# Depthwise convolution of a Conformer mixer: the shifted copies made by products with the identity, and all 31 taps on TensorE

## Chip, cores and metric

The kernel runs on one core of a Trainium2 chip. The metric is the device time of one execution, in microseconds (us). Engines: TensorE (PE; PEld is its weight load), VectorE (DVE), ScalarE (ACT), GpSimd (POOL) and SyncE (SP), which issues most DMAs. ScalarE has a DMA queue of its own.

## The reference

Two layers on 256 tokens of 2048 channels, float32. Layer 0 mixes the tokens by a state-space model, layer 1 by a causal convolution; each mixer is followed by a SwiGLU FFN of 5632 hidden units, each sub-layer by a layer norm, with scales, shifts and gates from a modulation `silu(c) @ ada_w`. The change lies in the convolution mixer:

```python
def conv_mixer(u, w_pw1, w_dw, b_dw, g_norm, b_norm, w_pw2):
    d = u.shape[-1]
    ab = u @ w_pw1
    v = ab[..., :d] * jax.nn.sigmoid(ab[..., d:])
    v = lax.conv_general_dilated(v, w_dw[:, None, :], window_strides=(1,),
        padding=((CONV_WIDTH - 1, 0),), dimension_numbers=('NWC', 'WIO', 'NWC'),
        feature_group_count=d) + b_dw          # CONV_WIDTH = 31
    v = layer_norm(v, g_norm, b_norm)
    return jax.nn.silu(v) @ w_pw2
```

Each channel is convolved with 31 taps of its own along the tokens; token t sees tokens t-30 to t.

## The kernel before

Activations lie as [channel, token], the channels in 16 chunks of 128. Even tokens come before odd ones, except in the convolution, which takes them in their order.

**Dense products.** A weight is taken in units of 512 rows by 512 columns (1 MB). SyncE's queue loads a unit into one of the four buffers of the pool `raw` (L496); ScalarE casts it into `whi` (L805), VectorE subtracts to get `wlo` (L806), and `gemm` (L811) makes 48 matmuls of 128x128 by 128x256 from it (L850): hi by hi, hi by lo, lo by hi. `whi` and `wlo` have two buffers each, so the cast of a unit waits until the products of the unit two before it are done. A panel is 256 output channels of both halves of `w_pw1`, four units; the mixer has eight panels. Panel 0 comes through a path of its own (`Entry`, L952), which also makes the input for the others.

**Work between the units.** `Later` (L565) holds work that is due some units on; `gemm` calls it ahead of each unit. `AdaQueue` (L618) puts loads of the modulation's weights, 1 MB each, between the units (0.6 a unit in this stage), and VectorE adds them up (L674).

**The convolution.** Behind each panel `conv_in` (L1427) takes its two chunks of gated channels: ScalarE copies a chunk to a padded buffer `pad` (L1431). The products need a tile `vs` in which 32 channels stand on all four quarters of the partitions, a token later on each: with it a 128x32 block of weights `lw` takes four taps at a time. The tile is made by a trip through DRAM: ScalarE's queue writes `pad` to the scratch tensor `scr` (L1433, 139.5 KB) and, when that is done, reads it back in overlapping rows into `vs` (L1440, 556.5 KB). GpSimd makes `lw` (L1442). `conv_out` (L1463) makes 4 x 6 products of 128x32 by 128x256 a chunk (L1467), four of them, for the four quarters of channels, into one PSUM bank; they hold taps 0 to 23. `conv_taps` (L1448) makes the last seven taps on VectorE (L1454 to L1458), and VectorE adds both to `V` (L1471) and, through `Stats`, to the sums of the layer norm (L748, L750; `lnsum` L765). `conv_taps` is put off by one unit and `conv_out` by three in most panels, longer in panels 0, 1 and 6.

**Around it.** PSUM has three banks in the pool `aux` (L498), which convolution, turns and sums share. The engines' instructions run in an order that the framework's scheduler sets when it builds the kernel. Behind the last panel, `fill` (L1509) gives TensorE products of the modulation while the layer norm is made; two of their loads are issued on ScalarE's queue behind the last `vs` load.

Of the kernel before, what the change touches and what calls it, by code (L numbers as in the profile page):

```python
# [26 lines left out]
CONV_G = 6  # groups of four taps of the convolution on the tensor engine  # L27
# [25 lines left out]
class Ops:  # L53
    """Short names for elementwise operations on one engine."""
# [27 lines left out]
    def exp(self, out, x):  # L82
        """out = e**x to float32, over the whole range of x."""
# [20 lines left out]
    def sincos(self, s_out, c_out, x):  # L104
        """s_out, c_out = sin(x), cos(x), x reduced by multiples of pi/2 in exact pieces."""
# [40 lines left out]
def bc(ap, axis, n):  # L146
    """The AP with a broadcast axis of length n put in at axis."""
    a = ap.unsqueeze(axis)
    sh = list(a.shape)
    sh[axis] = n  # L150
    return a.broadcast_to(sh)


class S5:
    """Parameter tables and the scan of the diagonal state-space mixer.

    Two tokens a step: H_c = a^2 H_{c-1} + (a B u_{2c} + B u_{2c+1}), and y = Re(C f H) with f = (a - 1) / lam.
    The complex state is kept in a frame that turns by 2*phi a step, phi the angle of a, in which the
    recurrence has the real factor |a|^2 and its two parts are two real scans.
    States lie on partitions as (group parity, n), group pairs along the free axis.  # L160
    """

    def __init__(self, tc, const, ident, psum, psum_tag, psum2):
# [5 lines left out]
        # B and C, the latter with -Im  # L169
        self.cm = self.keep.tile([P, 4, NPAIR, GI], F32, name="cm")  # L170
        # quarters of the channels of a tile, at both tokens of a step
# [22 lines left out]
    def load(self, pp, lam_re, lam_im, log_dt):  # L194
        """Pairs of groups on partitions, real parts on the first half of them."""
        nc = self.nc
        self.ld = pp.tile([64, 2], F32, name="ld")
        self.lam = pp.tile([P, P], F32, name="lam")
        self.nat = [pp.tile([P, 2 * NS * GI], F32, name=f"nat{i}") for i in range(2)]
        nc.sync.dma_start(self.ld, log_dt.rearrange("o (j a) -> (o j) a", a=2))  # L200
        for r, t in enumerate((lam_re, lam_im)):
            nc.sync.dma_start(self.lam[64 * r:64 * r + 64], t.rearrange("(j a) n -> j (a n)", a=2))
# [22 lines left out]
    def turn_mats(self):  # L225
        nc, cm = self.nc, self.cm
        # B and C, states to the partitions
# [14 lines left out]
    def prep(self, pp):  # L242
# [6 lines left out]
        # angles phi and phi * 4, 16, 64, the products by powers of two being exact  # L249
# [29 lines left out]
        # rotation factors e^{i 2 phi 2^j}, the first 16 steps of the tables, and |a|^2 e^{i 2 phi 64}  # L279
# [19 lines left out]
    def matrices(self, q, eng):  # L299
        """B, a B, C f and C f a of a quarter of the group pairs, in steps."""  # L300
# [5 lines left out]
        # (real or imaginary, pair, token of a step, channel) and (matrix, pair, channel)  # L306
# [20 lines left out]
    def quarter(self, q):  # L327
        """The first 32 steps of the tables of a quarter of the group pairs."""
# [6 lines left out]
    def double(self, t, w, j, xt, yt, npair, eng=None):  # L335
        """t[2^j : 2^{j+1}] = t[:2^j] * w along the last axis; t, w as [re, im]."""
# [15 lines left out]
    def tables(self, ct):  # L352
        """Rotation tables and decay factors of channel tile ct (4 group pairs) over 64 steps."""
# [15 lines left out]
    def weights(self, ct):  # L369
        """The matrices of channel tile ct in the shapes that the tensor engine takes."""  # L370
# [12 lines left out]
        # (pair, token of a step, channel) to the partitions, two pairs at a time  # L383
# [16 lines left out]
    def drive(self, ct, u):  # L400
        """PSUM banks with a B u_{2c} + B u_{2c+1}, two pairs of groups each; u by halves of the channels.

        Each pair takes half of the rows of the array, so that two products run at a time.
        """
# [9 lines left out]
    def scan(self, ct, banks, tab, between):  # L414
        """The states' real and imaginary parts as products of the scans with the tables.

        The frame starts anew after 64 steps; the state is carried over. between() is called where other
        work fits between operations that need one another.
        """
# [43 lines left out]
    def read_out(self, ct, u, pc, psn):  # L463
        """PSUM bank with y[ch, (tau, c)] of the channels of tile ct, without D u."""
# [3 lines left out]
        # Re(C H): C_re (c g_re - s g_im) - C_im (c g_im + s g_re)  # L468
# [15 lines left out]
def kernel(  # L484
# [4 lines left out]
    """Activations lie as [channel, token], tokens ordered (t mod 2, t div 2).  # L489

    Products with the weights are float32 products of operands split as hi + lo, each of 12 bits:
    hi hi + lo hi + hi lo, in one pass each.
    """
# [61 lines left out]
    def load_unit(src, k0, kn, segs, eng=nc.sync):  # L555
        """Rows of 128-chunks k0..k0+kn of a weight, column ranges segs (512 columns in all)."""
# [8 lines left out]
    class Later:  # L565
        """Work put off by some units of the dense products, so that the tensor engine needn't wait for its inputs."""
# [20 lines left out]
    def queue_behind(instructions):  # L587
        """A context whose instructions are issued after these, each on its own engine."""
# [8 lines left out]
    def ada_block(layer, j, q, behind={}):  # L597
        """Columns q*512.. of part j of the modulation, in four units; scales and gates get their 1 added."""
# [19 lines left out]
    class AdaQueue:  # L618
        """The rest of the modulation on the vector engine, a unit of 128 rows and 2048 columns at a time.

        parts = (layer, part, first of 4 blocks of 512 columns): what is left of a part from this block on;
        with half of the columns a unit has 256 rows.
        """
# [8 lines left out]
        def run(self, marks=()):  # L632
            """Adds up what was loaded before, behind these instructions."""
# [17 lines left out]
        def step(self):  # L651
            """Loads a unit; returns what adds it up."""
# [47 lines left out]
    def inverse_std(v, y, hv, t):  # L700
        """y = 1 / std from half of the variance, to which half of the epsilon is added; t for between.

        A first value from the exponent (negative), then three steps of Newton, each of which turns the sign.
        """
# [8 lines left out]
    class Stats:  # L713
        """Sums over the channels of z and z*z, z less the mean of its first 256 channels.

        Each quarter of the tokens has its sums on a quarter of the partitions. apart: the last two
        chunks stay out of the sums.
        """
# [5 lines left out]
        def begin(self, z):  # L724
            """z [128, 2, 256]: channel chunks 0 and 1; rewritten less the shift."""
# [10 lines left out]
        def add(self, i, z):  # L736
            """z [128, 2, 256]: channel chunks 2i and 2i+1, less the shift."""
# [17 lines left out]
        def finish(self, fill=None):  # L755
            """PSUM bank with 1/std and mean/std of z, on every partition.

            fill makes products for the tensor engine to do while it waits, in two steps.
            """
# [30 lines left out]
    def normal(z, r):  # L790
        """z [128, n, 256] -> (z - mean) / std in place."""
# [5 lines left out]
    class Unit:  # L797
        """A unit of a weight, loaded and split."""
# [769 lines left out]
```

## Time and profile before

| | |
|---|---|
| times of three runs | 2469.03, 2470.73, 2472.2 us (median 2470.73) |
| the profiled execution | span 2466.8 us from the first to the last instruction; no other time of it is recorded |
| busy | PE 2272.2 us (92%), DVE 1713.9 (69%), ACT 993.7 (40%), POOL 265.1 (11%) |
| mean granted TensorE clock | 0.963 |
| convolution's products (L1467) | 768 records, first at 1292.5 us, last at 1565.3 |
| taps on VectorE (L1454) | 96 instructions, median 484 ns |
| DMA issues of ScalarE's queue | 16 to `scr`, 16 to `vs` |
| moved | 584.36 MB, mean 237 GB/s |

How to read it: the page gives busy times by engine and by groups of instructions, with the idle time ahead of each and what ended it. The view of waits lists who waited for whom, with total, count and longest. The busy time by stretches gives the same for a window of the span. A float32 product of TensorE shows as two records.

### The profile page before, as it was taken

The page shows a single profiled execution, that of the slowest core. Times are in us where ns is not written, and L with a number is a line of the kernel's source. Part 1 is how long each engine was busy: PE and PEld are TensorE (multiplying, and loading weights), DVE is VectorE, ACT ScalarE, POOL GpSimd, SP SyncE. Part 2 cuts the span into 40 slices and gives each one's busy share as a digit, 9 for nine tenths or more (in the row PEclk, how much of TensorE's full clock was granted, in tenths as well). Part 3 has the DMA queues.
Part 4 walks back from the last instruction along what each step waited for, and adds up shares of the span by engine and source line. Part 5 has one row for each costly group of instructions (what it writes and reads, how often), then busy time and mean ns, then how long its engine had stood idle before and what let it go on. Part 6 is the DMA issues. An engine that isn't in the chain of part 4 may idle for free.

```text
span 2466.8 us, 46658 instructions
## 1 busy us (share of the span) xinstructions
PE 2272.2 (92%) x20224; PEld 2136.9 (87%) x20224; DVE 1713.9 (69%) x1884; ACT 993.7 (40%) x1191; POOL 265.1 (11%) x249
## 2 busy tenths in 40 slices
PE   5767899999999999999977867699999999999998
PEld 2434799999999999999976756499999999999998
DVE  8999888787776777778776564588765544545564
ACT  3555333564333334334452222345533333333343
POOL 3575200110000000000021100402000000000000
PEclk7888999999999999999989988899999999999999
DMA  9766899578888888888756676674775555555542
GB/s 293 252 222 200 308 344 339 189 265 299 307 306 300 302 303 300 305 315 287 242 167 180 186 193 174 226 256 155 254 263 185 187 188 180 182 187 188 188 158 100
DMA packets 377620, 584.36 MB, mean 237 GB/s; under 512 B 17315, under 2 KB 269523, under 8 KB 362819
## 3 DMA queue, kind: packets, MB, share of 16 engines
q1 hardware_dynamic: 371686, 567.43, 68.6%
q10 hardware_dynamic: 5520, 13.58, 2.0%
q8 instruction: 158, 2.59, 0.4%
q0 software_dynamic: 208, 0.37, 0.1%
q14 instruction: 48, 0.39, 0.0%
HBM read 576.95 MB, written 4.38 MB: 236 GB/s over the span
## 4 chain that ended last, share of the span: by engine, by line
PE 70%; DVE 12%; DMA 8%; issue 6%; ACT 2%; POOL 2%; ACTq 0%; SPq 0%; DVEq 0%; POOLq 0%
PE acc L850 66%; DMA raw<-in_cv_w_pw_dram 4%; DMA scr<-pad 2%; DVE x L433 1%; DMA vs<-scr 1%; DVE x L426 1%; DVE wlo L806 1%; ACT whi L805 1%; POOL hl L935 1%; DVE pc L458 1%; DMA raw<-in_s_w_glu_dram 1%; DVE adaacc L674 1%; POOL hf L1506 0%; DVE x L430 0%; DVE ct L1454 0%
## 5 line engine op out<-in xcount | busy, mean ns | idle before, releaser
L806 DVE TENSOR_TENSOR wlo<-raw,whi 128x2048 fp32r<-128x2048 f32 x344 | 792.0, 2302 | 595.0 <-ACT whi L805 590.7
L805 ACT CAST whi<-raw 128x2048 fp32r<-128x2048 f32 x344 | 655.8, 1907 | 977.8 <-PE acc L850 618.0
L850 PE MATMUL acc<-hh,whi 128*128 128x256 f32 x3904 | 668.0, 283 | 34.3 <-ACT whi L805 31.1
L850 PE MATMUL acc<-hl,whi 128*128 128x256 f32 x3904 | 664.1, 283 | 0.0
L850 PEld LDWEIGHTS acc<-hh,whi 128*128 128x128 f32 x3904 | 552.4, 190 | 55.2 <-ACT whi L805 36.7
L850 PEld LDWEIGHTS acc<-hl,whi 128*128 128x128 f32 x3904 | 550.6, 190 | 1.0 <-issue 0.8
L850 PE MATMUL acc<-hh,wlo 128*128 128x256 f32 x3904 | 514.6, 282 | 4.4 <-DVE wlo L806 4.4
L850 PEld LDWEIGHTS acc<-hh,wlo 128*128 128x128 f32 x3904 | 485.8, 190 | 5.4 <-DVE wlo L806 5.4
L674 DVE SCALAR_TENSOR_TENSOR adaacc<-rawa,c_act,adaacc 128x2048 f32<-128x2048 f32 (+1 forms) x135 | 286.3, 2121 | 0.3
L850 PE MATMUL acc<-fh,whi 128*128 128x256 f32 x1408 | 237.5, 284 | 0.0
L850 PE MATMUL acc<-fl,whi 128*128 128x256 f32 x1408 | 236.7, 283 | 0.0
L850 PEld LDWEIGHTS acc<-fh,whi 128*128 128x128 f32 x1408 | 199.0, 192 | 0.9 <-ACT whi L805 0.8
L850 PEld LDWEIGHTS acc<-fl,whi 128*128 128x128 f32 x1408 | 198.9, 192 | 0.0
L850 PE MATMUL acc<-fh,wlo 128*128 128x256 f32 x1408 | 185.9, 283 | 0.0
L850 PEld LDWEIGHTS acc<-fh,wlo 128*128 128x128 f32 x1408 | 176.4, 192 | 0.0
L1442 POOL TENSOR_TENSOR lw<-fold,wtap 128x768 f32<-128x768 f32 x16 | 31.4, 1962 | 967.6 <-PE acc L850 721.2
L1467 PE MATMUL conv<-vs,lw 128*32 128x256 f32 x768 | 55.7, 450 | 62.6 <-DMA vs<-scr 62.6
L1467 PEld LDWEIGHTS conv<-vs,lw 128*32 128x32 f32 x768 | 28.5, 128 | 85.3 <-issue 63.8
L604 PE MATMUL ada<-raw,c_rep 128*32 128x512 f32 x512 | 79.8, 704 | 6.6 <-DMA raw<-in_ada_w_dram 6.5
L935 POOL TENSOR_TENSOR hl<-hf,hh 128x512 fp32r<-128x512 f32 x24 | 47.9, 2007 | 284.4 <-ACT hh L934 277.2
L1094 POOL CAST lnmh<-lno 128x2 fp32r<-128x2 f32 x1 | 0.2, 183 | 725.1 <-DVE lno L65 725.1
L1148 ACT ACTIVATE fsg<-acc 128x256 f32<-128x256 f32 x84 | 32.0, 381 | 108.4 <-PE acc L850 108.4
(318 smaller groups left out, 1705.3 us busy)
## 6 DMA issues: line engine op xcount, KB each, us to landing
raw<-in_ffn_w_gu_dram SPq DMA_DIRECT2D x352, 512.0 KB
rawa<-in_ada_w_dram SPq DMA_DIRECT2D x128, 1024.0 KB
raw<-in_ffn_w_down_dram SPq DMA_DIRECT2D x88, 1024.0 KB
raw<-in_ada_w_dram SPq DMA_DIRECT2D x62, 1024.0 KB
raw<-in_s_w_glu_dram SPq DMA_DIRECT2D x64, 512.0 KB
raw<-in_cv_w_pw_dram SPq DMA_DIRECT2D x64, 512.0 KB
raw<-in_cv_w_pw_dram SPq DMA_DIRECT2D x16, 1024.0 KB
vs<-scr ACTq DMA_DIRECT2D x16, 556.5 KB
```

The source lines that it names most:

```text
L426: v.tensor_tensor(out=dst.rearrange("p r s a c -> p a (r s) c")[:, a::2], in0=pv.rearrange("p a r (s c) -> p a (r s) c", s=2), in1=bc(f[:, ...
L433: v.tensor_tensor_scan(out=x2[:, r, s].rearrange("p a c -> p (a c)"), data0=rh.rearrange("p a c -> p (a c)"), data1=x1[:, r, s].rearrange( ...
L458: v.tensor_tensor(out=pc[:, r].rearrange("p a (s c) -> p s a c", s=2), in0=x2[:, r], in1=bc(t[:, 0], 1, 2), op=MUL)
L604: nc.tensor.matmul(acc[32 * k:32 * k + 32, :], c_rep[:, 4 * u + k, :], r[:, k, :], start=u == 0, stop=u == 3)
L674: nc.vector.scalar_tensor_tensor(out=acc, in0=r[:, i], scalar=c_act[:, kk:kk + 1], in1=acc, op0=MUL, op1=ADD)
L805: m1 = nc.scalar.copy(out=self.hi[:, :kn], in_=r[:, :kn])
L806: m2 = nc.vector.tensor_tensor(out=self.lo[:, :kn], in0=r[:, :kn], in1=self.hi[:, :kn].bitcast(F32), op=SUB)
L850: nc.tensor.matmul(acc[bank][:, i], wt[:, k, m * P:(m + 1) * P], xx(u0 + k), start=u == 0 and n == 0 and i == 0, stop=last and n == len(or ...
L935: nc.gpsimd.tensor_tensor(out=hl[:, s2], in0=h, in1=hh[:, s2].bitcast(F32), op=SUB)
L1148: nc.scalar.activation(out=t[:, i], in_=gv[:, 0], func=AF.Sigmoid)
L1442: nc.gpsimd.tensor_tensor(out=lw, in0=fold32.unsqueeze(1).unsqueeze(1).broadcast_to([P, 4, CONV_G, 32]), in1=bc(wtap[:, :, 4 * ch:4 * ch + ...
L1467: nc.tensor.matmul(acc[32 * q:32 * q + 32, :], lw[:, q, g, :], vs[:, LS * q + 4 * g:LS * q + 4 * g + SEQ], start=g == 0, stop=g == CONV_G - 1)
```

## The change

`CONV_G` becomes 8, so that the products take all 31 taps (the 32nd is zero) and `conv_taps` goes. The scratch tensor goes with both DMAs of each chunk. In their place `conv_spread` multiplies, for each quarter of the channels, 32 columns of the identity by the padded chunk at four shifts, each into a quarter of the partitions of a bank of `aux`, 284 tokens long; ScalarE copies the banks of two quarters to `vs`, VectorE those of the other two. The delays become one unit for `conv_spread` and two for `conv_out` (one more for a panel's second chunk), in every panel. `vs` has three buffers for four, `lw` three for two. All loads of `fill` go to SyncE's queue. The taps' table `wtap` is 8 groups wide; the table for VectorE, `vtap`, goes.

```diff
-CONV_G = 6  # groups of four taps of the convolution on the tensor engine
+CONV_G = 8
...
-        LS = 4 * CONV_G - 1 + SEQ
-        dramp = mctx.enter_context(tc.tile_pool(name="dram", bufs=1, space=bass.MemoryType.DRAM))
+        LS = 4 * CONV_G - 4 + SEQ
...
         def conv_in(i, t):
             p = pad[i % 2]
-            scr = []
             for k in range(2):
                 nc.scalar.copy(out=p[:, k, WIDTH - 1:LP - 1].rearrange("p (c t) -> p t c", t=2), in_=t[:, k].rearrange("p (t c) -> p t c", t=2))
-                scr.append(dramp.tile([32, 4, LS], F32, name=f"scr{2 * i + k}"))
-                m = nc.scalar.dma_start(scr[k].rearrange("c q t -> q c t"), p[:, k, 0:LS])
             for k in range(2):
                 ch = 2 * i + k
-                vs = cp.tile([P, 4 * LS - 3], F32, tag="vs", name="vs", bufs=4)
-                flat = scr[k].rearrange("c q t -> c (q t)")
-                with queue_behind([m]):
-                    loads.append(nc.scalar.dma_start(vs, bass.AP(flat.tensor, flat.offset, [[1, 4], [4 * LS, 32], [1, 4 * LS - 3]])))
-                lw = cp.tile([P, 4, CONV_G, 32], F32, tag="lw", name="lw", bufs=2)
+                vs = cp.tile([P, 4, LS], F32, tag="vs", name="vs", bufs=3)
+                lw = cp.tile([P, 4, CONV_G, 32], F32, tag="lw", name="lw", bufs=3)
...
-                later.put((5 if i == 6 else 4 if i == 1 else 1) + k, lambda ch=ch, z=p[:, k]: conv_taps(ch, z))
-                later.put((6 if i == 6 else 5 if i < 2 else 3) + k, lambda ch=ch, lw=lw, vs=vs: conv_out(ch, vs, lw))
-
-        def conv_taps(ch, p):
...
+                later.put(1 + k, lambda z=p[:, k], vs=vs: conv_spread(z, vs))
+                later.put(2 + k, lambda ch=ch, lw=lw, vs=vs: conv_out(ch, vs, lw))
+
+        def conv_spread(z, vs):
+            for q in range(4):
+                b = aux("spread")[:, :LS]
+                for j in range(4):
+                    nc.tensor.matmul(b[32 * j:32 * j + 32, :], ident[:, 32 * q:32 * q + 32], z[:, j:j + LS], start=True, stop=True)
+                if q % 2 == 0:
+                    nc.scalar.copy(out=vs[:, q], in_=b)
                 else:
...
+                    nc.vector.tensor_copy(out=vs[:, q], in_=b)
...
-            nc.vector.scalar_tensor_tensor(out=o, in0=a, scalar=cb_col[:, ch:ch + 1], in1=d, op0=ADD, op1=SUB)
             if ch < 2:
+                nc.vector.tensor_scalar(out=o, in0=a, scalar1=cb_col[:, ch:ch + 1], scalar2=None, op0=ADD)
...
+            nc.vector.scalar_tensor_tensor(
+                out=o, in0=a, scalar=cb_col[:, ch:ch + 1], in1=cstats.shift.rearrange("p (t c) -> p c t", t=2), op0=ADD, op1=SUB)
...
-            blocks = [ada_block(1, 5, 0, {u: loads[-1:] for u in (2,3,)}), ada_block(1, 5, 1)]
+            blocks = [ada_block(1, 5, 0), ada_block(1, 5, 1)]
```

The order of the instructions moves with it. On TensorE, at the start of a panel in the middle of the mixer (panel 3; `adat` is a turn of the modulation), before:

```order
L850 MATMUL acc<-hh,wlo 128x256 x8
L1467 MATMUL conv<-vs,lw 32x256 x24
L690 MATMUL adat<-ident,adas 128x128 x4
L850 MATMUL acc<-hh,whi 128x256 x4
L850 MATMUL acc<-hl,whi 128x256 x4
```

and now, at the start of the same panel's second unit:

```order
L850 MATMUL acc<-hh,wlo 128x256 x16
L1451 MATMUL conv<-vs,lw 32x256 x32
L1441 MATMUL spread<-pad_13248,ident 32x284 x16
L850 MATMUL acc<-hh,whi 128x256 x4
L850 MATMUL acc<-hl,whi 128x256 x4
```

Where a unit was followed by one chunk's convolution (of the panel before), it is now followed by a longer one and by the products that spread the next chunk; the first chunk's spread stands ahead of the panel's first unit or early in it.

On ScalarE, from the gate (`sg`) of one panel on, before (one chunk's `pad`, its DMA to `scr`, then the DMAs to `vs`, with casts between them):

```order
L1013 ACTIVATE sg<-acc 128x256
L1431 COPY pad_13254<-sg 128x2x128
L1433 DMA scr_14904<-pad_13254 4x32x279
L805 CAST whi<-raw 128x2048
L1013 ACTIVATE sg<-acc 128x256
L1431 COPY pad_13254<-sg 128x2x128
L1433 DMA scr_14907<-pad_13254 4x32x279
L1440 DMA vs<-scr_14904 128x1x1113
L805 CAST whi<-raw 128x2048
L1440 DMA vs<-scr_14907 128x1x1113
```

and now (a panel earlier):

```order
L1013 ACTIVATE sg<-acc 128x256
L1425 COPY pad_13248<-sg 128x2x128
L805 CAST whi<-raw 128x2048
L1013 ACTIVATE sg<-acc 128x256
L1443 COPY vs<-spread 128x284 x2
L1425 COPY pad_13248<-sg 128x2x128
L805 CAST whi<-raw 128x2048
L1443 COPY vs<-spread 128x284 x2
L805 CAST whi<-raw 128x2048
```

The four DMA issues are gone; in their place stand two pairs of copies out of PSUM, the first pair behind one cast and the second gate, the second pair behind another cast.

More of the change, by code (lines that the diff above doesn't have):

```diff
@@ L1280, in start_dense @@
             ready.append(Unit(wp, s5_w_glu[0], 4 * u, 4, [(0, 256), (D, 256)]))
-    const2 = wp = ln_col = wtap = vtap = fold32 = row_of = None
+    const2 = wp = ln_col = wtap = fold32 = row_of = None
     with tc.manual_schedule(engines={mybir.EngineType.PE}):
@@ L1337, in load_vectors @@
             t = sp.tile([P, 2, SEQ], F32, tag="hf", name="rt", bufs=2).rearrange("p a b -> p (a b)")[:64].rearrange("p (k c) -> p k c", c=32)
-            n = min(16, 4 * CONV_G - 16 * h)
+            n = min(16, WIDTH - 16 * h)
+            if n < 16:
+                nc.gpsimd.memset(t[:, n:], 0.0)
             nc.gpsimd.dma_start(t[:, :n], cv_w_dw[0, 16 * h:16 * h + n].rearrange("k (a c) -> a k c", c=32))
             rt.append(t)
-        vt = rows_in("vtap", [rows_of(cv_w_dw[0, 4 * CONV_G:])], nc.gpsimd)
         row_of = const2.tile([P, 4, P], F32, name="row_of")
@@ L1348, in load_vectors, with turn_vectors @@
             nc.gpsimd.tensor_tensor(out=fold32, in0=ident[:, 0:32] if i == 1 else fold32, in1=ident[:, 32 * i:32 * i + 32], op=ADD)
-        later.put(4, lambda: turn_vectors(ab, ln, rt, vt))
-    def turn_vectors(ab, ln, rt, vt):
-        nonlocal ln_col, wtap, vtap
+        later.put(4, lambda: turn_vectors(ab, ln, rt))
+    def turn_vectors(ab, ln, rt):
+        nonlocal ln_col, wtap
         ab_col.append(turned_rows("adab1", ab, const2))
@@ L1358, in turn_vectors @@
         wtap = const2.tile([P, CONV_G, 64], F32, name="wtap")
-        t = turned_rows("vtap", vt, const2)
-        nc.vector.tensor_scalar(out=t, in0=t, scalar1=-1.0, scalar2=None, op0=MUL)
-        vtap = t.rearrange("p (k c) -> p k c", c=NCH)
         b = aux("wt")
@@ L1423 @@
         cstats = Stats("cln", sp)
-        taps, loads = {}, []
         ada.rate = 0.6
@@ L1444, in conv_in @@
                     in1=bc(wtap[:, :, 4 * ch:4 * ch + 4].rearrange("p g q -> p q g"), 3, 32), op=MUL)
-                later.put((5 if i == 6 else 4 if i == 1 else 1) + k, lambda ch=ch, z=p[:, k]: conv_taps(ch, z))
-                later.put((6 if i == 6 else 5 if i < 2 else 3) + k, lambda ch=ch, lw=lw, vs=vs: conv_out(ch, vs, lw))
-        def conv_taps(ch, p):
-            d = cp.tile([P, SEQ], F32, tag="ct", name="ct", bufs=3)
-            for j in range(4 * CONV_G, WIDTH):
-                w, z = vtap[:, j - 4 * CONV_G, ch:ch + 1], p[:, j:j + SEQ]
-                if j > 4 * CONV_G:
-                    nc.vector.scalar_tensor_tensor(out=d, in0=z, scalar=w, in1=d, op0=MUL, op1=ADD)
-                elif ch < 2:
-                    nc.vector.tensor_scalar(out=d, in0=z, scalar1=w, scalar2=None, op0=MUL)
-                else:
-                    nc.vector.scalar_tensor_tensor(
-                        out=d.rearrange("p (c t) -> p c t", t=2), in0=z.rearrange("p (c t) -> p c t", t=2), scalar=w,
-                        in1=cstats.shift.rearrange("p (t c) -> p c t", t=2), op0=MUL, op1=ADD)
-            taps[ch] = d
+                later.put(1 + k, lambda z=p[:, k], vs=vs: conv_spread(z, vs))
[7 more added lines that the diff above has]
+                    nc.scalar.copy(out=vs[:, q], in_=b)
+                else:
+                    nc.vector.tensor_copy(out=vs[:, q], in_=b)
         def conv_out(ch, vs, lw):
@@ L1467, in conv_out @@
                     nc.tensor.matmul(
-                        acc[32 * q:32 * q + 32, :], lw[:, q, g, :], vs[:, LS * q + 4 * g:LS * q + 4 * g + SEQ], start=g == 0, stop=g == CONV_G - 1)
-            d = taps.pop(ch).rearrange("p (c t) -> p c t", t=2)
+                        acc[32 * q:32 * q + 32, :], lw[:, q, g, :], vs[:, q, 4 * g:4 * g + SEQ], start=g == 0, stop=g == CONV_G - 1)
             o, a = V[:, ch].rearrange("p (t c) -> p c t", t=2), acc.rearrange("p (c t) -> p c t", t=2)
-            nc.vector.scalar_tensor_tensor(out=o, in0=a, scalar=cb_col[:, ch:ch + 1], in1=d, op0=ADD, op1=SUB)
             if ch < 2:
+                nc.vector.tensor_scalar(out=o, in0=a, scalar1=cb_col[:, ch:ch + 1], scalar2=None, op0=ADD)
                 if ch == 1:
```

## The prediction

> **What bounds the kernel now.** The page first: the kernel is a stream of products on TensorE. The second row gives forty equal slices of the span, 61.7 us each; TensorE's busy digit is 9 nearly everywhere, but for the start and five slices a little past the middle.
>
> ```profile
> span 2466.8 us, 46658 instructions
> PE   5767899999999999999977867699999999999998
> ```
>
> Those slices (the 21st to the 25th) are the convolution mixer, so the next view is the busy time by stretches. The first row runs from the first matmul of panel 2 (panels are counted from 0, eight in all) to the start of the sums of the layer norm behind the convolution; the second is a stretch of layer 0's FFN, for comparison. Columns: start and end, length, busy time of PE, PEld, DVE, ACT and POOL with their counts, granted clock, share of the DMA engines, GB/s.
>
> ```profile
> 1280.40:1567.30 286.90, 201.13 (x1941) 171.25 (x1940) 159.23 (x189) 65.49 (x70) 27.66 (x14) 0.85 0.66 179
> 1160.00:1220.00 60.00, 60.00 (x502) 60.00 (x501) 45.75 (x42) 24.70 (x22) 0.00 (x0) 1.00 0.80 278
> ```
>
> TensorE does nothing for 286.9 - 201.1 = 85.8 us of this stage and gets 0.85 of its clock; in the FFN it is full, at clock 1.00, while DMA moves 278 GB/s against 179 here. Neither VectorE (159) nor ScalarE (65) is near its limit. Who is waited for, in the same stretch:
>
> ```profile
> ACT whi L805 <- DMA raw<-in_cv_w_pw_dram: 107.5, 8, 23.0
> PE conv L1467 <- DMA vs<-scr: 62.6, 7, 13.1
> ACT whi L805 <- DMA scr<-pad: 22.0, 3, 16.9
> PE acc L850 <- ACT whi L805: 18.1, 2, 17.0
> ```
>
> TensorE itself waits for the copies that come back from DRAM (62.6 us) and for cast weights (18.1). But behind the first wait stands a second one: ScalarE waits 107.5 us for the weights of the same panels. The queues, over this stretch and over one panel, tell why:
>
> ```profile
> DMA  9952002379999999999999999322227999722322
> GB/s 351 361 199 80 8 10 42 61 171 312 198 199 197 221 226 221 189 217 193 216 188 231 192 245 230 89 92 100 102 105 198 237 283 289 283 101 103 119 103 98
> ...
> q1 hardware_dynamic: 25551, 37.81, 48.3%
> q10 hardware_dynamic: 5146, 13.36, 16.8%
> ```
>
> (The first two rows are 1500 to 1535 us in forty slices, the other two the stage.) q10 is ScalarE's queue with the copies, q1 SyncE's with the weights. Near the end of that panel the engines sit at a share of 2 to 3 tenths and about 100 GB/s: a quarter of the sixteen works, the rest are done. I read this as copies that lie on four engines: their 16.8% of sixteen is 67% of those four, and with q1's 48.3% these are past 100%, so the weights, spread over all, wait for the crowded ones. [...]
>
> **What TensorE's own work is worth.** From the timeline of TensorE (start, length, instruction, count):
>
> ```profile
> 1280.41 0.64 PE L850 MATMUL acc<-hh,whi 128*128 128x256 f32 x4
> ...
> 1301.37 2.80 PE L1467 MATMUL conv<-vs,lw 128*32 128x256 f32 x48
> 1304.10 0.74 PE L850 MATMUL acc<-hh,whi 128*128 128x256 f32 x4
> 1304.68 0.64 PE L850 MATMUL acc<-hl,whi 128*128 128x256 f32 x4
> 1305.16 0.64 PE L850 MATMUL acc<-hh,whi 128*128 128x256 f32 x4
> ...
> 1309.88 1.03 PE L728 MATMUL shift<-V,ones_m 128*128 128x256 f32 x4
> 1310.56 0.83 PE L850 MATMUL acc<-hh,whi 128*128 128x256 f32 x4
> ...
> 1316.51 1.06 PE L682 MATMUL adar<-adaacc,ones 128*32 128x512 f32 x8
> 1317.51 0.50 PE L850 MATMUL acc<-hh,whi 128*128 128x256 f32 x2
> ...
> 1329.65 1.11 PE L690 MATMUL adat<-ident,adas 128*128 128x128 f32 x4 [3.48 <-ACT adas L684]
> 1330.41 1.20 PE L850 MATMUL acc<-hh,whi 128*128 128x256 f32 x4
> 1331.41 1.05 PE L850 MATMUL acc<-hl,whi 128*128 128x256 f32 x4
> ...
> 1567.28 0.64 PE L765 MATMUL lnsum<-cln_s,ones 128*32 128x128 f32 x16 [1.60 <-DVE cln_s L748]
> ...
> 1619.22 0.64 PE L850 MATMUL acc<-hh,whi 128*128 128x256 f32 x4
> 1624.91 0.64 PE L850 MATMUL acc<-hh,whi 128*128 128x256 f32 x4
> ```
>
> A unit of the dense product (48 matmuls) takes 1624.91 - 1619.22 = 5.69 us when nothing is late. The 24 products of the convolution of one channel chunk (two records each) take 1304.10 - 1301.37 = 2.73 us, 0.114 us a product. The first group behind it starts the next 0.58 us later, where 0.48 is usual (1304.68 to 1305.16): 0.10 us for the change from column tiles to the full array. Small ones: the total of the modulation 1.00 (1316.51 to 1317.51), its turn 0.76 (1329.65 to 1330.41), the shift 0.68 (1309.88 to 1310.56).
>
> From 1280.41 to 1567.28, 286.9 us, TensorE has panels 2 to 7 (24 units, 136.6), 16 chunks of convolution (43.7), 16 such changes (1.6), the small ones (2.4): 184.3. So 102.6 us are lost: 85.8 idle and 16.8 by matmuls at a lower clock behind a wait (four take 1.05 us at 1331.41, 0.64 otherwise).
>
> **The change, part by part.** The whole round trip goes: 32 DMAs, both waits. ScalarE's queue no longer stands behind them, and the weights have SyncE's queue and all engines to themselves: q1's 48.3% of 287 us is 139 us, well under the new length of the stage, and in the FFN the weights keep up with TensorE at 278 GB/s. So I take all 102.6 us as won, and count what TensorE gets in their place.
>
> Products with the identity: 16 chunks x 4 quarters x 4 shifts = 256, each 32 columns wide and 284 tokens long, of the convolution's kind: 0.114 x 284/256 = 0.126 us, 32.3 us in all. Taps 24 to 30 on TensorE: 8 groups for 6, 128 products more, 14.6 us. Sixteen more blocks of column tiles between full ones, 0.10 us each: 1.6 us. [...]
>
> Copies out of PSUM: 64 new ones of 128x284, half on ScalarE, half on VectorE. VectorE loses the taps. The rows, by shape in the stage (the page's line for 128x384 is the nearest copy on VectorE):
>
> ```profile
> L805 ACT CAST whi<-raw 128x2048 fp32r<-128x2048 f32 x24 | 45.6, 1904 | 146.5 <-DMA raw<-in_cv_w_pw_dram 107.5 <-DMA scr<-pad 22.0 <-PE acc L850 10.3
> L806 DVE TENSOR_TENSOR wlo<-raw,whi 128x2048 fp32r<-128x2048 f32 x24 | 56.3, 2348 | 81.3 <-ACT whi L805 81.3
> L1454 DVE SCALAR_TENSOR_TENSOR ct<-pad,vtap,ct 128x256 f32<-128x256 f32 x93 | 45.6, 515 | 1.5
> L899 ACT ACTIVATE X<-X,m1xb,m1xg 128x256 f32<-128x256 f32 x9 | 4.7, 589 | 1.0 <-ACT pad L1431 1.0
> L1013 ACT ACTIVATE sg<-acc 128x256 f32<-128x256 f32 x13 | 4.9, 378 | 11.6 <-PE acc L850 6.3 <-DMA scr<-pad 5.3
> L684 ACT COPY adas<-adar 128x512 f32<-128x512 f32 x1 | 0.6, 579 | 0.0
> L730 ACT COPY shift<-shift 128x256 f32<-128x256 f32 x1 | 0.4, 358 | 0.0
> ...
> L1365 DVE COPY wtap<-wt 128x384 f32<-128x384 f32 x1 | 0.6, 550 | 0.0
> ```
>
> A copy on ScalarE lies between 0.36 (256 wide) and 0.58 (512): 0.39; on VectorE it is under 0.55 (384 wide): 0.41, by its width. A chunk's two copies on an engine take under 1 us while its 16 products take 2.0, so throughput is no limit; VectorE does some 107 x 0.5 us of taps less. What costs is the place of the copies in a queue that runs in order. A chunk has four quarters but three banks; the fourth quarter waits until ScalarE has copied the first. In the new order ScalarE has one cast of weights and one sigmoid ahead of that copy where a panel begins, and that cast cannot start before TensorE has done the last unit of the panel before: 1.90 + 0.38 + 0.39 - 3 x 0.50 (three quarters of products) = 1.2 us, on six panels 7.2. The second chunk's copies come behind a cast too, but TensorE runs the first chunk's convolution meanwhile: 32 x 0.114 = 3.6 us cover it, and without that cover it would be the same 1.2. At the first pair nine activations of X (4.7 us by the row) are ahead of the second chunk's copies, with nothing on TensorE that doesn't need them: 4.4. At the end no dense product hides the last two chunks' copies: 2 x 1.0, and VectorE's way into the sums, 1.6 as before (the wait at 1567.28), with some slack 4.0. Together 15.6 us of waits; bounds from 4 (the end alone) to twice as much.
>
> Nothing else is on the path: GpSimd's weights grow from 768 to 1024 columns but are made a panel ahead; the two modulation loads that move from ScalarE's queue to SyncE's stand behind the last panel's weights, in the place where their neighbours already stand, so nothing new waits for them.
>
> Sum: -102.6 + 32.3 + 14.6 + 1.6 + 15.6 = -38.5 us. The span 2466.8, all that is recorded of the profiled execution's time, becomes 2428.3. The median of the runs (2470.7) lies 3.9 us over the span, so 2432.2, say 2432. The stage should last 248 us and TensorE be the one waited for.
>
> **Rivals.** (1) The copies out of PSUM bind: each of the 14 later chunks waits for a cast and a subtraction (1.90 + 2.35 - 1.5 = 2.7 us), 38 in place of 7.2: 2463. For it: three banks for four quarters, and both engines' queues run in order. Against: VectorE and ScalarE are idle for much of the stage (159 and 65 of 287). [...] (2) Slower: the products with the identity don't run four at a time. Then each would take what a full-width one does: two took 0.68 us at the shift, and the next group was 0.19 late (0.83 for 0.64), so 0.43 each, 0.48 for 284 tokens; 256 x (0.48 - 0.126) = 91 more, 2523. It decides from 0.275 us a product upwards. Against: the convolution's products write the same four quarters of one bank from one row group, and take 0.114. (3) Slower: the weights are late for a reason other than the copies, as by buffers that VectorE frees late; then the 102.6 us stay and 48.5 of products and changes of mode come on top: 2519; slower from 54 us of loss that remain. For it: the row of 107.5 us. Against: the FFN with the same ring of buffers shows none, at a higher rate.
>
> **How the numbers follow.** Forecast 0.79, with 2419 (waits of 4, free changes of mode) to 2448 (waits doubled) as its own range; rival 1 0.12, rival 2 0.03, rival 3 0.06. The range goes to 2455, halfway into rival 1. A measurement of this kernel can tell about 0.2% (5 us) from no change; rival 1 with a little more lands there, so same has 0.02, slower 0.09, faster 0.89.
>
> **What would show it.** In the new profile: no q10 but a sliver; the stretch of panels 2 to 7 near 248 us with TensorE busy over 90% and clock near 1; spread groups of 32 records in 2.0 us, convolutions of 64 records in 3.6; waits of spread products for ScalarE's copies of about 1 us, once a panel; ScalarE's casts waiting for TensorE and not for the weights' DMA. I am wrong if casts still wait tens of us for weights (rival 3), if 32 records take over 4 us (rival 2), or if the waits for copies come to more than 30 us (rival 1).

## The result and the profile after

The changed kernel takes 2404.2 us (median; 2401.85 to 2409.69 in four runs), the kernel before 2471.47 in the same session (2469.03 to 2473.62): a ratio of 0.9729, 95% interval 0.9712 to 0.9745. The forecast was 2432 with a range of 2419 to 2455. The direction and the stage were right, the size was not: 67 us came where 38.5 were worked out. Times of the runs further on are medians of four executions; one of e4's took 6843.01 us, for a reason that nothing here shows, and e4's median is over the other three.

From the page of the changed kernel, the span, TensorE's forty slices and ScalarE's DMA queue:

```profile
span 2399.6 us, 48120 instructions
PE   5777899999999999999999999899999999999998
q10 hardware_dynamic: 240, 0.08, 0.0%
```

The five weak slices are gone, and so is the queue of the copies, but for a sliver. The mixer from the start of panel 1 to the sums of the layer norm, and below it the part from panel 2 on, with the products with the identity that lead it (columns as in the prediction):

```profile
1243.64:1509.00 265.36, 260.14 (x2898) 210.38 (x2897) 150.32 (x138) 99.05 (x138) 42.19 (x20) 0.99 0.51 167
1285.10:1509.00 223.90, 221.53 (x2509) 178.65 (x2509) 122.56 (x106) 70.10 (x86) 26.70 (x11) 1.00 0.53 175
```

From panel 2 on TensorE is idle for 2.4 us of 223.9, at clock 1.00; before, 85.8 of 286.9, at 0.85. (The lengths are not to be set against one another, since the convolutions of the first two chunks now lie ahead of panel 2; the marks below serve for that.) The waits of the mixer after, from panel 1 on:

```profile
ACT whi L805 <- PE acc L850: 56.5, 24, 4.4
ACT vs L1443 <- PE spread L1441: 38.1, 23, 4.7
...
PEld spread L1441 <- ACT vs L1443: 4.3, 8, 0.6
...
PEld spread L1441 <- DVE V L1460: 3.1, 6, 0.7
```

No cast waits for weights any more; the casts and the copies out of PSUM wait for TensorE, and TensorE waits for ScalarE's copies only 4.3 us in all, never over 0.6 at a time.

But the stage is not where all of the gain is. Two marks that both traces have are the last group of layer 0's down projections (first row; after, then before) and the sums behind the convolution:

```profile
1216.07 1.12 PE L850 MATMUL acc<-fh,wlo 128*128 128x256 f32 x8
...
1509.02 0.64 PE L765 MATMUL lnsum<-cln_s,ones 128*32 128x128 f32 x16 [1.57 <-DVE cln_s L748]
```

```profile
1226.61 1.12 PE L850 MATMUL acc<-fh,wlo 128*128 128x256 f32 x8
```

So the changed kernel is already 10.5 us ahead before the mixer begins, gains 47.7 between the marks (1567.28 - 1226.61 = 340.67 against 292.95), and 8.9 more behind them (2466.8 - 1567.28 = 899.5 against 890.6). But for the loading and turning of the table of taps and the two loads of `fill`, nothing of the change runs in the first of these stretches or the last. What is different there shows when two neighbouring units of the same dense product are laid side by side; the last groups of two units of layer 0's FFN, before:

```profile
913.21 2.06 PE L850 MATMUL acc<-hh,wlo 128*128 128x256 f32 x16
918.90 2.06 PE L850 MATMUL acc<-hh,wlo 128*128 128x256 f32 x16
```

and after:

```profile
905.93 1.98 PE L850 MATMUL acc<-hh,wlo 128*128 128x256 f32 x16
911.49 1.98 PE L850 MATMUL acc<-hh,wlo 128*128 128x256 f32 x16
```

A unit of 48 products takes 5.69 us before and 5.56 after, with no idle time in either: 118.5 and 115.8 ns a product. In the down projections, whose moving operand is fh or fl, the pace is 120.0 ns in both kernels.

### The profile page after: what moved, and what is told of

Read it like the earlier page. It is cut to its first block, busy times and chain, and to the rows that moved or that the text cites. A ratio compares the mean times of both kernels' runs of the same rounds, so it can differ in the third digit from the quotient of the medians.

```text
span 2399.6 us, 48120 instructions
## 1 busy us (share of the span) xinstructions
PE 2285.2 (95%) x20993; PEld 2130.4 (89%) x20993; DVE 1682.0 (70%) x1802; ACT 1006.2 (42%) x1223; POOL 270.4 (11%) x249
## 4 chain that ended last, share of the span: by engine, by line
PE 78%; DVE 12%; issue 5%; ACT 2%; POOL 2%; DMA 1%; SPq 0%; DVEq 0%; ACTq 0%; POOLq 0%
PE acc L850 73%; PE conv L1451 2%; DVE x L433 2%; DVE pc L458 1%; DVE x L426 1%; ACT whi L805 1%; POOL hl L935 1%; PE spread L1441 1%; DVE wlo L806 1%; DMA raw<-in_s_w_glu_dram 1%; DVE adaacc L674 1%; DVE u L1259 0%; DVE x L430 0%; DVE x L429 0%; POOL hf L1491 0%
## 5 line engine op out<-in xcount | busy, mean ns | idle before, releaser
L850 PE MATMUL acc<-hh,whi 128*128 128x256 f32 x3904 | 658.0, 281 | 15.3 <-ACT whi L805 13.3
L850 PEld LDWEIGHTS acc<-hh,whi 128*128 128x128 f32 x3904 | 544.0, 188 | 38.6 <-ACT whi L805 18.0
L850 PE MATMUL acc<-hh,wlo 128*128 128x256 f32 x3904 | 499.7, 278 | 4.5 <-DVE wlo L806 4.5
L850 PEld LDWEIGHTS acc<-hh,wlo 128*128 128x128 f32 x3904 | 472.0, 188 | 7.2 <-DVE wlo L806 5.4
L1430 POOL TENSOR_TENSOR lw<-fold,wtap 128x1024 f32<-128x1024 f32 x16 | 37.6, 2357 | 893.3 <-PE acc L850 713.1
L1451 PE MATMUL conv<-vs,lw 128*32 128x256 f32 x1024 | 61.5, 381 | 0.3 <-DVE vs L1445 0.3
L454 POOL TENSOR_TENSOR psn<-x,tab 128x512 f32<-128x512 f32 x32 | 49.7, 1567 | 64.2 <-DVE x L433 59.9
```

Of the source, the lines that this page charges most:

```text
L454: self.last = nc.gpsimd.tensor_tensor(out=psn[:, r].rearrange("p a (s c) -> p s a c", s=2), in0=x2[:, r], in1=bc(t[:, 1], 1, 2), op=MUL)
L850: nc.tensor.matmul(acc[bank][:, i], wt[:, k, m * P:(m + 1) * P], xx(u0 + k), start=u == 0 and n == 0 and i == 0, stop=last and n == len(or ...
L1430: nc.gpsimd.tensor_tensor(out=lw, in0=fold32.unsqueeze(1).unsqueeze(1).broadcast_to([P, 4, CONV_G, 32]), in1=bc(wtap[:, :, 4 * ch:4 * ch + ...
L1451: nc.tensor.matmul(acc[32 * q:32 * q + 32, :], lw[:, q, g, :], vs[:, q, 4 * g:4 * g + SEQ], start=g == 0, stop=g == CONV_G - 1)
```

## The experiments

One thing that the change does in passing offers itself. The table of taps grows from 6 to 8 groups (1536 to 2048 bytes a partition) and the 448 bytes of the taps for VectorE go, so the pool of small vectors is 64 bytes longer, and every pool behind it, with the cast weights whi and wlo at its head, lies 64 bytes further on (whi at 113280 before, 113344 after). hh and hl lie ahead of that pool and stay (38272 and 54784); fh and fl lie behind it and move with the weights. **Theory L**: the place of the weights against the moving operand sets the pace. **Rival O**: the pace comes from another order of the instructions.

**e1_before_pad64** is the kernel before with 64 unused bytes:

```diff
-        fold32 = const2.tile([P, 32], F32, name="fold32")
+        fold32 = const2.tile([P, 48], F32, name="fold32")[:, 0:32]
```

> The kernel before with one unused 64 bytes a partition in the pool of small vectors (a tile of 32 columns made 48 wide): every instruction and its order are those of before, but the cast weights whi and wlo, and everything behind them, lie 64 bytes further on, where they lie in the changed kernel. Theory L (part of the gain is where the weights lie against the moving operand hh): products with hh in the rows of casts go from 118.5 ns to 115-116 ns apart, those with fh and fl stay at 120.0, and the time falls by 15 to 22 us, to about 2452 us. Rival O (the gain outside of the mixer comes from another order of instructions): nothing changes, 2471 us.

Measured: 2457.42 us, ratio 0.9937 (0.9922 to 0.9952), 15 us less, with the same instructions in the same order; units with hh are 5.56 us apart in its trace. **e2_after_unpad64** is the reverse, the changed kernel with the old places (one small operation on VectorE moves, all else keeps its order):

```diff
-        t = const2.tile([P, NCH], F32, name=name)
+        t = const2.tile([P, NCH], F32, tag="f0xb" if name == "f1xb" else name, name=name)
```

> The changed kernel with two small vectors of 64 bytes sharing one place, so that whi, wlo and all behind them lie where they lay before the change; one small operation on VectorE moves. Theory L: products with hh are 118.5 ns apart again and the time rises by about 20 us, to 2424 us, which is what is left of the change alone. Rival O: 2404 us.

Measured: 2425.61 us, ratio 0.9807 (0.9793 to 0.9822), 21.4 us more than the changed kernel. The same pair of groups in its trace is 5.69 us apart again:

```profile
909.29 2.06 PE L850 MATMUL acc<-hh,wlo 128*128 128x256 f32 x16
914.98 2.06 PE L850 MATMUL acc<-hh,wlo 128*128 128x256 f32 x16
```

Rival O falls. By the three stretches of the profiled executions (worked out from the same two marks of each trace and its span):

| us | to the mark | mixer | behind it | span |
|---|---|---|---|---|
| before | 1226.6 | 340.7 | 899.5 | 2466.8 |
| e1, 64 bytes added | 1215.2 | 349.3 | 890.5 | 2454.9 |
| e2, change without the 64 bytes | 1228.4 | 294.4 | 902.5 | 2425.3 |
| after | 1216.1 | 293.0 | 890.6 | 2399.6 |
| e3, copies cut in four | 1228.0 | 294.0 | 903.5 | 2425.5 |
| e4, taps on VectorE | 1216.6 | 280.9 | 893.0 | 2390.5 |

In e1 the mixer takes 8.6 us more. TensorE is busy there for 2.1 us less (249.9 us, before 252.0), but it is idle for 10.6 us more (99.3, before 88.7), most of it for the copies (72.5 us, before 62.6); that is why the gain is 15 and not 21. Why these waits grow by more than the products gain was not found. The change without its 64 bytes brings 46.3 us between the marks, and nothing elsewhere (the two other stretches are 1.8 and 3.0 us longer).

**m1_offsets** measures the disputed effect by itself. Products only, each `nc.tensor.matmul(a, W[:, k, 128*m:128*m+128], X[:, d//4:d//4+256])` for 16 values of d:

> Not the computation (the output is a constant): only products of the dense kind, 96 for each of 16 distances between the moving operand and one fixed tile of weights (moved by 0 to 768 bytes), each product with its own weight load, three times: with nothing beside them, then with VectorE and ScalarE streaming 128x2048 operands in SBUF, then with weights arriving by DMA. Theory L1 (the distance decides by itself, through reads of moving operand and weights that meet): the time from one product to the next differs by 2 to 5 ns between distances in all three sweeps, with the distances of before (0 modulo 256) slow and those of after (64, that is a move by 192) fast. Theory L2 (the distance matters only against what other engines and DMAs do at the time): the first sweep is flat within 1 ns, and a difference shows in the second or third only, or not at all if it hangs on things that are not here.

The timeline, from the first sweep (a number in the name is d in bytes; W lies 5120 bytes behind X, so the weights lie -d behind the moving operand modulo 256), and one distance of the second and the third:

```profile
54.92 11.47 PE L68 MATMUL a64x<-X,W 128*128 128x256 f32 x96
66.23 11.68 PE L68 MATMUL a96x<-X,W 128*128 128x256 f32 x96
...
100.40 11.06 PE L68 MATMUL a192x<-X,W 128*128 128x256 f32 x96
111.30 11.52 PE L68 MATMUL a224x<-X,W 128*128 128x256 f32 x96
122.65 11.68 PE L68 MATMUL a256x<-X,W 128*128 128x256 f32 x96
134.17 11.47 PE L68 MATMUL a320x<-X,W 128*128 128x256 f32 x96
...
281.74 11.06 PE L68 MATMUL c192x<-X,W 128*128 128x256 f32 x96
292.64 11.52 PE L68 MATMUL c224x<-X,W 128*128 128x256 f32 x96
...
463.08 11.06 PE L68 MATMUL e192x<-X,W 128*128 128x256 f32 x96
473.98 11.52 PE L68 MATMUL e224x<-X,W 128*128 128x256 f32 x96
```

From the start of one row to the start of the next are 96 products: (111.30 - 100.40) / 96 = 113.5 ns where the weights lie 64 bytes behind modulo 256, (134.17 - 122.65) / 96 = 120.0 at 0, 117.8 at 192 (54.92 to 66.23); from the trace also 118.6 at 128, 118.2 at 32, 117.4 at 96. Distances 256 apart agree, and but for the very first 96 products the three sweeps agree within 0.2 ns, whether nothing else runs, or VectorE and ScalarE stream operands (busy 107 and 105 us of 130), or weights arrive at 318 GB/s. So it is L1 as far as the distance goes: in these sweeps it alone sets the pace, 113.5 to 120.0 ns. L1's reads that meet were the author's guess; how the distance acts was not shown. hh stood at 0 and stands at 64 after the change; hl went from 128 to 192; fh and fl are at 0 in both. Two of three products of a unit take hh, one takes hl, so by this table the mean would go from 119.5 to 114.9 ns. The kernels show 118.5 and 115.8: the direction is the table's, the size is 2.7 ns and not 4.6, and what makes the difference was not taken apart.

What of the lost 102.6 us came from the crowded engines? **e3_before_split16** cuts each copy of the kernel before into four DMAs of 32 partitions:

```diff
-                m = nc.scalar.dma_start(scr[k].rearrange("c q t -> q c t"), p[:, k, 0:LS])
+                for q in range(4):
+                    m = nc.scalar.dma_start(scr[k][:, q], p[32 * q:32 * q + 32, k, 0:LS])
...
-                    loads.append(nc.scalar.dma_start(vs, bass.AP(flat.tensor, flat.offset, [[1, 4], [4 * LS, 32], [1, 4 * LS - 3]])))
+                    for j in range(4):
+                        loads.append(nc.scalar.dma_start(vs[32 * j:32 * j + 32], bass.AP(flat.tensor, flat.offset + j, [[4 * LS, 32], [1, 4 * LS - 3]])))
```

> The kernel before, taps and trip through DRAM kept, with each of the two copies of a channel chunk cut into four DMAs of 32 partitions (one for each quarter). Theory C (the copies crowd onto four of the sixteen DMA engines, and the weights wait for those four): they spread over all engines, the plateau of 2 to 3 tenths at 100 GB/s goes, casts stop waiting for weights, and the stage of panels 2 to 7 falls from 287 us to 195-220 us (TensorE's own work is 184 us, and the DMA share of 0.65 over 287 us is 187 us of all engines): 2390 to 2405 us. Rival (the latency of two DMAs one behind the other and of ScalarE's blocked queue): the stage stays above 260 us and the time above 2445 us.

Measured: 2424.61 us, ratio 0.9805 (0.9791 to 0.982). Its waits between 1280 and 1522 us:

```profile
PE conv L1469 <- DMA vs<-scr: 33.5, 9, 7.1
...
ACT whi L805 <- DMA vs<-scr: 31.6, 3, 11.3
...
ACT whi L805 <- DMA raw<-in_cv_w_pw_dram: 14.5, 3, 10.7
```

The share of the DMA engines over the same panel as in the prediction (here 1470 to 1505 us) no longer has the plateau:

```profile
DMA  9587979999999999831000000000058999991132
```

The wait of casts for their weights falls from 107.5 us to 14.5, so the crowding was real, and the mixer gains 46.7 us: as much as the whole change without its 64 bytes (e2). That a smaller DMA also lands sooner by itself is not separated from this. The time lies between what theory C and its rival expected: from the first convolution on the stage takes 236.2 us (1285.80 to 1522.04), where theory C had 195 to 220; the trip's own waits remain, TensorE's for the copies (33.5 us) and ScalarE's, whose casts stand in its queue behind copies that wait (31.6). Crowding was about half of the loss, not all. **e7_before_split16_pad64** adds e1's 64 bytes to e3:

> The kernel before, with copies cut into four DMAs each and the 64 unused bytes. If the two causes are separate, their gains add: 2424.6 - 15 to 21 = 2404 to 2410 us, as fast as the changed kernel without one product with the identity. If the faster products outside the mixer are lost to its copies and weights, 2415 us or more.

Measured: 2404.53 us, ratio 0.9729 (0.9707 to 0.975). The two causes add, and this equals the changed kernel without one product with the identity.

The halves of the change. **e8_before_taps_on_tensor** is the kernel before with `CONV_G = 8` and no `conv_taps`; **e4_after_taps_on_vector** is the changed kernel with `CONV_G = 6` and `conv_taps` put back.

> Half of the change: all 31 taps on TensorE, trip through DRAM kept (weights lie where they lie in the changed kernel, so the comparison is the kernel before with 64 unused bytes, 2457 us). Theory C (the mixer is bound by its copies on four DMA engines, and TensorE has idle time to hide 14.6 us of products): 2457 us, up to 5 us more for copies that are 3% longer. Rival (the products come on top): 2472 us. Rival (VectorE's taps were a part of the lateness): under 2450 us.

Measured: 2460.49 us, ratio 0.9961 (0.9946 to 0.9976), 3 us over e1, which has the same places. The taps alone gain nothing: between 1240 and 1570 us of that trace TensorE waits 81.1 us for copies, more than the 62.6 of the kernel before.

> The changed kernel with only taps 0 to 23 on TensorE and taps 24 to 30 on VectorE as before (the identity products stay; the weights lie where they lie in the changed kernel). Theory B (the stage is bound by TensorE's own work now): 128 products of 0.114 us and 2.9% of the identity products less, 2404 - 15.5 = about 2389 us. Rival (VectorE's 7 taps of 0.5 us stand ahead of its copies out of PSUM in its queue, and TensorE waits for these): each chunk loses up to 2 us, and the time is 2400 us or more.

Measured: 2391.51 us, ratio 0.9668 (0.9649 to 0.9688), 12.7 us under the changed kernel, with 12.0 of its profiled execution in the mixer. With the spread on TensorE the taps do lie on the path, and this half of the change costs time. Some 3 of the 15.5 us did not come; that VectorE's fuller queue took them was not tried.

**e6_after_spread_twice** doubles the disputed cost (`for j in list(range(4)) * 2` around the products with the identity):

> The changed kernel with every product with the identity issued twice into the same place (the result is the same). If the stage is bound by TensorE and four of them run at a time, as priced: 256 x 0.126 = 32 us more, 2436 us (2432 to 2442). If the copies out of PSUM hide part of them: under 2425 us. If they run one at a time at 0.48 us: over 2500 us.

Measured: 2431.41 us, ratio 0.9841 (0.9824 to 0.9857), 27.2 us more: 0.106 us a product, where four at a time were priced at 0.126 and one at a time at 0.48. Some 5 us of the 32 did not come; the 4.3 us for which the changed kernel's spread waits for ScalarE's copies have no row in this trace, so the second set covers them. Rival 2 of the prediction (91 us) is out.

The table of distances says more than the change used: fh and fl stand at the slowest place (0, 120.0 ns). **f1_after_fh_moved** puts 192 unused bytes ahead of them:

```diff
-                fp = f0ctx.enter_context(tc.tile_pool(name="f0", bufs=1, reuse_waits="tile"))
+                fp = f0ctx.enter_context(tc.tile_pool(name="f0", bufs=1, reuse_waits="tile")); fp.tile([P, 48], F32, name="gap")
```

(and the same for the pool f1.)

> The changed kernel with 192 unused bytes a partition ahead of fh and fl, the moving operands of the down projections (all orders of instructions as in the changed kernel), so that the weights lie 64 bytes behind them modulo 256, as they do for hh there, where it was 0. By the table of distances (120.0 ns at 0, 113.5 at 64) and 4224 such products (2 layers x 44 x 16 x 3): 27 us less, about 2377 us, and 113 to 115 ns for them in the trace. Rival (the down projections wait for weights as soon as products are faster): 2390 us or more.

Measured: 2387.64 us, ratio 0.9658 (0.964 to 0.9675): 16.6 us less, not 27. In its timeline two pairs of neighbouring units, all at one distance:

```profile
740.26 2.05 PE L850 MATMUL acc<-fh,wlo 128*128 128x256 f32 x16
745.91 2.05 PE L850 MATMUL acc<-fh,wlo 128*128 128x256 f32 x16
...
808.99 1.98 PE L850 MATMUL acc<-fh,wlo 128*128 128x256 f32 x16
814.43 1.98 PE L850 MATMUL acc<-fh,wlo 128*128 128x256 f32 x16
```

5.65 us a unit (117.7 ns), later 5.44 (113.3). Four units on end, from 740.26 to 762.87 us, keep the first pace, nine, from 798.11 to 847.07, the second. Both occur at this one distance, so the distance does not ensure the fast pace.

**f2_taps_on_vector_all_moved** is e4 with fh and fl moved so, and hl brought to the same distance:

```diff
-    hh_all, hl_all = (const.tile([P, NCH * EW], F32R, name=n) for n in ("hh", "hl"))
+    hh_all, hl_all = (const.tile([P, NCH * EW + 32], F32R, name=n)[:, 0:NCH * EW] for n in ("hh", "hl"))
```

> The changed kernel with taps 24 to 30 on VectorE, fh and fl moved as in the last, and hl moved by 128 bytes so that it stands to the weights as hh does. From 2392 us: 27 us for fh and fl, and 4096 products of hl at 118.7 - 114.5 = 4.2 ns, 17 us: about 2348 us. If hh,whi products gain too, since they alternate with those of hl (116.2 to 114), 9 us more: 2339. Rival (weights' arrival binds): 2365 us or more.

Measured: 2341.78 us, ratio 0.9475 (0.9447 to 0.9503), 50 us under e4. In its profiled execution, the fastest of the four, the first down projections run at the fast pace (four units on end from 731.85 to 753.61 us, 5.44 each); over the whole span the mean matmul of fh and whi takes 277 ns, 279 in f1 and 284 in the changed kernel:

```profile
731.85 1.98 PE L850 MATMUL acc<-fh,wlo 128*128 128x256 f32 x16
737.29 1.98 PE L850 MATMUL acc<-fh,wlo 128*128 128x256 f32 x16
```

Last, the trip through DRAM with all that was learnt: e7 with these places, its copies on GpSimd's queue in **f4_before_split16_pool_queue_all_moved** and on ScalarE's in **f5_before_split16_act_queue_all_moved**; between these two only `nc.gpsimd.dma_start` and `nc.scalar.dma_start` differ.

> The trip through DRAM with copies cut into four DMAs each, issued on GpSimd's queue in place of ScalarE's, and the three operands placed as in the last. By places alone: 2404.5 - 44 = 2360 us. Theory Q (what is left of the waits there is ScalarE's queue, where casts stand behind copies that wait for one another, 32 us): 2335 to 2350 us. Rival (the latency of the trip is what is left, or GpSimd issues slowly): 2358 us or more.

> As the run before it, but with the copies on ScalarE's queue again; one thing is different between the two. Placing alone brought 50 us in the changed kernel with taps on VectorE (2392 to 2342). Theory Q (ScalarE's queue is worth what is left, casts no longer stand behind copies that wait): here 2354 to 2360 us, 22 us or more above the 2332 us on GpSimd's queue. Rival (the queue is worth nothing and the placing did it all): 2330 to 2340 us.

Measured: f4 2332.37 us, ratio 0.9421 (0.9392 to 0.945); f5 2353.81, 0.9549 (0.9503 to 0.9594). f5 is where placing alone should be, so the 21 us between them go with the queue; f4 is a little under what theory Q expected. The two paces blur this number: by the marks of the profiled executions the mixer takes 270.6 us in f4 and 295.2 in f5, 24.6 less, but the rest of the span takes 11.3 us more in f4, whose units between 512 and 648 us are 5.65 us apart where f5's are 5.44. From 1240 to 1510 us, the casts of f5 wait for copies that stand ahead of them in the queue, the first row; in f4 there is no such row, and they wait for their weights at most, the second:

```profile
ACT whi L805 <- DMA vs<-scr: 45.2, 4, 13.0
```

```profile
ACT whi L805 <- DMA raw<-in_cv_w_pw_dram: 40.0, 5, 10.7
```

f4 is the fastest of all, beyond f2, the fastest with the identity; their intervals touch.

## Why the prediction was right and wrong

- **Right: what the stage loses, and that it all comes back.** "I take all 102.6 us as won": from panel 1 on 5.2 us of 265.4 are idle after the change (265.36 - 260.14), at clock 0.99. The reason given, copies on four engines, was about half of it (e3: 46.7 us), and that they are four was read from the share of 2 to 3 tenths, since no view shows the engines one by one; ScalarE's blocked queue was another part (24.6 us of the mixer between f5 and f4). The rest of the trip's waits was not taken apart. The change removes the whole trip, so the sum did not feel this.
- **Right: the price of TensorE's new work.** 32.3 us for the identity stand against 27.2 for a second set of them (e6); 14.6 for the taps against 12.7 (e4, of 15.5 with the shorter spread). A group of 32 records holds TensorE for 2.06 us (1392.30 to 1394.36, below), where 2.0 was forecast. The changes of mode of the range and of rival 3, from column tiles to the full array, cost 0.10 us again: behind a spread a group of four starts the next 0.57 us later (1299.30 to 1299.87), where 0.47 is usual (1390.45 to 1390.92).
- **Wrong in size: "Together 15.6 us of waits".** Without the 64 bytes the change brings 46.3 us in the mixer (46.8 in the medians), where 38.5 were forecast. If the other terms are as they were, waits of 7.8 are left; that is a remainder, in which their errors lie too. The largest term was the one for panel starts: "that cast cannot start before TensorE has done the last unit of the panel before: 1.90 + 0.38 + 0.39 - 3 x 0.50 = 1.2", 7.2 on six panels. The trace shows 2.0 on the six together, at most 0.62 on one. Panel 5 begins so, on ScalarE:

```profile
1389.75 1.90 ACT L805 CAST whi<-raw 128x2048 fp32r<-128x2048 f32 x1 [1.54 <-PE acc L850]
1391.56 0.38 ACT L1013 ACTIVATE sg<-acc 128x256 f32<-128x256 f32 x1
1391.84 0.42 ACT L1425 COPY pad<-sg 128x256 f32<-128x256 f32 x1
1393.06 0.40 ACT L1443 COPY vs<-spread 128x284 f32<-128x284 f32 x1 [0.81 <-PE spread L1441]
```

  and on TensorE:

```profile
1389.51 1.10 PE L850 MATMUL acc<-hh,wlo 128*128 128x256 f32 x8
1390.45 0.64 PE L850 MATMUL acc<-hh,whi 128*128 128x256 f32 x4
...
1391.86 0.40 PE L850 MATMUL acc<-hl,whi 128*128 128x256 f32 x2
1392.30 2.12 PE L1441 MATMUL spread<-pad,ident 128*32 128x284 f32 x32
1394.36 0.50 PE L850 MATMUL acc<-hl,whi 128*128 128x256 f32 x2
```

  A unit's last products use wlo, so whi comes free before the unit ends, and the cast starts 0.70 us before the next unit (1390.45). That unit's first 14 products then run ahead of the spread (to 1392.30, 1.85 us). ScalarE is done 2.55 us earlier than assumed and waits 0.81 us for the first quarter, in place of being waited for. The sum gave this cast no cover, and here it had two. On four of the six panels the spread stands ahead of the first unit, so that only the early cast is left, and TensorE's weight loads wait 0.18 to 0.62 us. Panel 2 is one of them (first row; the other two are its second chunk):

```profile
1286.82 0.16 PEld L1441 LDWEIGHTS spread<-pad,ident 128*32 128x32 f32 x8 [0.58 <-ACT vs L1443]
...
1297.92 0.16 PEld L1441 LDWEIGHTS spread<-pad,ident 128*32 128x32 f32 x8 [0.62 <-ACT vs L1443]
1298.68 0.16 PEld L1441 LDWEIGHTS spread<-pad,ident 128*32 128x32 f32 x8 [0.60 <-DVE V L1460]
```

  The second chunks were taken as covered; their spreads wait 1.8 us in all for ScalarE's copies and 3.1 for a bank that VectorE's addition to `V` still reads. The 4.4 us of the first pair did not come: the activations of X (first row) stand ahead of the copies as was said, but TensorE had the first chunk's convolution to do meanwhile (second row):

```profile
1267.18 4.55 ACT L899 ACTIVATE X<-X,m1xb,m1xg 128x256 f32<-128x256 f32 x9
```

```profile
1268.05 3.21 PE L1451 MATMUL conv<-vs,lw 128*32 128x256 f32 x52
```

  At the end, with 4.0 forecast, TensorE waits 0.5 us for ScalarE's copies, 0.6 for VectorE's and 1.6 ahead of the sums.

- **The step that failed most, by omission: "Nothing else is on the path".** The sum was made over the stage alone, and the rest of the span was taken as unchanged. The 64 bytes that the tables grew by changed the pace of the dense products with hh all over the kernel: 21.4 us (e2 against after), most of the 28 by which the forecast missed, and what took the time out of the range; without them it was 2425.6 (e2), inside. The unit that was priced as 5.69 us from the row at 1619.22 is 5.56 in the changed kernel.
- The sum with both terms mended: -38.5 - 7.8 - 21.4 = -67.7; measured -67.3. Since the 7.8 is a remainder, that the sum closes proves nothing about the waits; the 21.4 is a measurement.
- **The rivals.** None came: copies out of PSUM bind little (4.3 us of waits, where rival 1 had 38), identity products cost 0.106 us each (e6), where rival 2 had 0.48, and from panel 1 on no cast waits for its weights.

## What to carry to other kernels

Before crediting a change with its gain, look at stretches that it does not touch: a gain there has another cause, and one kernel with only that cause (here 64 unused bytes) tells them apart. A DMA that crowds a few engines is first to be cut so that it spreads, and taken off a queue that others stand in, before compute is spent to replace it: here the cut alone bought as much as 256 products with the identity (e7 2404.53 us, the changed kernel 2404.2), and with the other queue 2332.37 (f4) stands against 2341.78 with the identity (f2). Work that moved onto the engine that bounds cost nearly its full time here (12.7 us of 15.5), so the half of a change that does so is tried without.

## What the hardware showed that was not expected

- In m1 the pace of 128x256 products with a weight load each hangs on where the weights lie against the moving operand, modulo 256 bytes: 113.5 ns with the weights 64 bytes behind, 120.0 at 0, 116.7 to 120.0 at the other distances tried. VectorE and ScalarE, busy 107 and 105 us of 130, and DMA at 318 GB/s changed it by under 0.2 ns. How this comes about was not taken apart.
- With the weights 64 bytes behind, two paces were measured, 113.3 and 117.7 ns (f1: nine and four units on end; f4: 5.65 us a unit from 512 to 648 us, where f5 has 5.44). What sets which one was not found.
- Places alone brought f2 50 us of e4's 2392, with every instruction and its order the same.
